# A hybrid decoder trunk with expert retrieval on one core: gate tiles laid out in token pairs, the two routing blocks interleaved, gate steps spread, GpSimd subtractions moved

## The chip, the core and the metric

The kernel runs on one core of a Trainium2 chip. The metric is the device time of one execution in microseconds (us); a time given for a kernel is the median of its runs. The profile is one execution taken by the hardware profiler. Its engines are PE (TensorE: matmuls; PEld is its weight loads), DVE (VectorE), ACT (ScalarE), POOL (GpSimd) and SP (which issues DMAs). Each engine works through its own queue in the order of the program and waits on semaphores for the others.

## What is computed

The network has two layers over 256 tokens of width 1024. Each layer is a token-mixing sublayer (a recurrent, a state-space and an attention group side by side) and a channel-mixing sublayer, the expert retrieval, each followed by a LayerNorm. The change touches the retrieval alone:

```python
def chunk(xc):                                   # 128 tokens
    q = (xc @ wq).reshape(c, PEER_HEADS, 2, half)
    sc = jnp.einsum('thid,ikd->thik', q, keys)   # 8 heads, 2 halves, 128 keys each
    top_s, top_i = lax.top_k(sc, 16)
    cand_s = top_s[:, :, 0, :, None] + top_s[:, :, 1, None, :]
    cand_i = top_i[:, :, 0, :, None] * 128 + top_i[:, :, 1, None, :]
    best_s, best_pos = lax.top_k(cand_s.reshape(c, 8, -1), 16)
    idx = jnp.take_along_axis(cand_i.reshape(c, 8, -1), best_pos, axis=-1)
    gate = jax.nn.softmax(best_s, axis=-1)
    act = gelu(jnp.einsum('td,thkd->thk', xc, u[idx]))
    return jnp.einsum('thk,thkd->td', gate * act, v[idx])
```

So every token picks 8 x 16 of 16,384 experts; the result is the sum over the chosen experts of gate x gelu(x . u) x v.

## The kernel before, in words

The kernel does not gather experts. It computes x . u for all 16,384 of them (the **u stretch**: 128 weight pieces of 128 experts), multiplies by a gate array that is zero where an expert was not chosen, and multiplies by all of v (the **v stretch**: 128 pieces). The array `act` holds [128 first keys, 128 second keys, 256 tokens].

**Weight pieces.** Each piece is 128 x 1024 float32. `pump_split` splits it into a high part `hi` (ACT, L117) and a low part `lo = raw - hi` (L118), up to two pieces ahead (`LOOK`), in three buffers each. L118 stands on DVE, or on POOL for the pieces in the set `on_pool` (L92). A piece of the u stretch is 24 matmuls (`proj_T`, recorded at L193), eight times hi x hTh, hi x hTl and lo x hTh, into one half of a PSUM bank; after two pieces `uevac` applies the GELU on ACT (L977, L980) and, for tokens whose gates are already in place, the product on DVE (L978).

**Background work.** After each u piece the loop takes one or two steps of generators, in this order: routing of token block 0, routing of token block 1, `wgen`.

- `routing(tb)` finds the top 16 of 128 scores for 8 heads x 2 halves (16 searches, L846 to L850), builds 112 candidates per head (L876 to L880), searches them (8 searches), and then makes the choice: exponentials and small index arithmetic (L887 to L903), two one-hot products of 128 x 2048 bf16 (L907 on ACT, L909 and L913 on DVE), 16 small matmuls each, and the transposed key numbers `ijT` and gates `gT`. These are 40 steps.
- `wgen` builds the gate array four tokens at a time (64 groups). `gates` compares key numbers with an iota (L937), multiplies by the gate (L940), and scales a copy (L942), all in half floats on DVE. `wmm` then takes, for each of the four tokens, two 128 x 128 x 128 matmuls (8 in a group), and `apply` puts the result into `act` (DVE L956 for pieces already computed, ACT L958 for the others). A group's gates, matmuls and application stand in three steps that follow each other.

In `eq` and `ga` the four tokens of a group lie next to each other, so the 128 keys that one matmul reads are 4 half floats (8 bytes) apart: `eq[:, 1, :, i]` of a tile [128, 2, 128, 4].

**Order.** The code order is the priority; the framework places each instruction in its engine's queue by that and by its data, so DVE's routing work stands further ahead than the loop's steps say. PE's queue keeps the order of the code. The v stretch begins with `gsplit` of the first four pieces of `act` (ACT L1011, DVE L1012), which write into the buffers of `eq` and `ga`.

Of the kernel before, what the change touches and what calls it, by code (L numbers as in the profile page):

```python
# [16 lines left out]
D = 1024  # L17
# [29 lines left out]
def trunk(ctx, tc, x, wst, ut, vr, pp_d, rb_d, lnrow, bd_d, keys_d, out):  # L47
# [42 lines left out]
    for l in range(DEPTH):  # L90
        on_pool.update(index["w", l, i] for i in (0, 1, 14, 16, 18, N_IN + N_OUT, N_IN + N_OUT + 1))
        on_pool.update(index["u", l, j] for j in range(4, 110, 3))  # L92
# [57 lines left out]
    iota4 = const.tile([128, 128, 4], F16, name="iota4")  # L150
# [19 lines left out]
    def make_consts():  # L170
        POOL.iota(iota4, pattern=[[1, 128], [0, 4]], base=0, channel_multiplier=0, allow_small_or_imprecise_dtypes=True)
# [135 lines left out]
    # (step, token block, part): r residual and sums, m mean and squares, v variance, n reciprocal root, s centre and  # L307
    # gain, o scale and bias with the transposes, l low halves, p the next weight pieces
# [50 lines left out]
    def log1p_exp_neg_abs(pool, o, xin, n, tag):  # L359
        """o = max(x, 0) + log1p(exp(-|x|)) on [128, n]"""  # L360
        a = pool.tile([128, n], F32, name=tag + "_a")
        e = pool.tile([128, n], F32, name=tag + "_e")
        q = pool.tile([128, n], F32, name=tag + "_q")
        ACT.activation(a, xin, AF.Abs)
        ACT.activation(e, a, AF.Exp, scale=-1.0)
        DVE.tensor_scalar(a, e, 2.0, None, op0=OP.add)
        DVE.reciprocal(a, a)
        DVE.tensor_tensor(e, e, a, op=OP.mult)
        DVE.tensor_tensor(a, e, e, op=OP.mult)
        DVE.tensor_scalar(q, a, 1.0 / 17.0, None, op0=OP.mult)  # L370
# [22 lines left out]
    def mixer(l, mix, h, hT, pre):  # L393
# [6 lines left out]
        # small per-layer values  # L400
# [31 lines left out]
        # causal depthwise convolution  # L432
# [293 lines left out]
        # projection schedule  # L726
# [60 lines left out]
        # output projection  # L787
# [33 lines left out]
    def peer(l, pool, hT):  # L821
        hTh, hTl = hT
        act = pool.tile([128, 128, SEQ], F32, name="act")
        ijT = pool.tile([128, 2, SEQ], F16, name="ijT")
        gT = pool.tile([128, 2, SEQ], F16, name="gT")
# [26 lines left out]
        def routing(tb):  # L852
# [19 lines left out]
            for hh in range(8):  # L872
                for i in range(2):
                    top16(tv[:, hh, i, :], ti[:, hh, i, :], sc[:, hh, i, :])
                    yield
# [8 lines left out]
            for hh in range(8):  # L884
                top16(bs[:, hh, :], bp[:, hh * 16:hh * 16 + 16], cand[:, hh, :])
                yield
            DVE.tensor_tensor(ex, bs, bs[:, :, 0:1].to_broadcast([128, 8, 16]), op=OP.subtract)  # L887
# [17 lines left out]
            ts = slice(tb * 128, (tb + 1) * 128)  # L905
            for i in range(2):
# [12 lines left out]
                ACT.activation(ijT[:, i, ts], ps, AF.Copy)  # L919
# [4 lines left out]
            ACT.activation(gT[:, 0, ts], ps, AF.Copy, scale=GS)  # L924
            DVE.scalar_tensor_tensor(gr, ps, GS, gT[:, 0, ts], op0=OP.mult, op1=OP.subtract)
            ACT.activation(gT[:, 1, ts], gr, AF.Copy, scale=LS)
            yield

        state = dict(c=0, t=0)
        TG = 4  # L930
        GS, LS = float(2 ** 15), float(2 ** 11)
# [29 lines left out]
        def wgen():  # L961
            prev = {}
            ng = SEQ // TG
            for i in range(ng + 2):
# [4 lines left out]
                if i >= 2:  # L969
                    apply((i - 2) * TG, prev.pop(i - 2))  # L970
                yield
# [10 lines left out]

        bg = Background()
        bg.add(routing(0))
        bg.add(routing(1))
        bg.add(wgen())
        for jp_ in range(64):
# [7 lines left out]
        # second product  # L995
        po = [[acc_bank() for _ in range(2)] for _ in range(2)]
        early = [[pool.tile([128, w], F32R, name=nm, bufs=2)[:, 0:2 * SEQ] for _ in range(2)]
                 for nm, w in (("eq", 512), ("ga", 768))]
# [151 lines left out]
```

## Time and profile before

| what | value |
|---|---|
| median of 3 runs | 2103.95 us (2101.63 to 2104.25) |
| span of the profiled execution | 2106.6 us |
| PE, PEld busy | 96 %, 87 % |
| DVE, ACT, POOL busy | 73 %, 50 %, 11 % |
| u stretch of layer 0 | 254.46 to 706.42 us |
| u stretch of layer 1 | 1297.10 to 1748.89 us |

Busy shares are means over the whole span; stretches differ. The u stretch has three parts: the routing part (pieces 0 to 53), the gate part (pieces 54 to 117, one group of gates with each piece) and ten pieces without background work. A matmul's record lasts longer than its place in the stream, since matmuls are pipelined: the distance from one start to the next is what a matmul costs.

### The profile page before, as it was taken

How to read it: one execution, taken by the hardware profiler on the slowest of the kernel's cores; microseconds unless marked ns; L12 is line 12 of the kernel's file. 1: busy time of each engine (PE TensorE's matmuls, PEld its weight loads, DVE VectorE, ACT ScalarE, POOL GpSimd, SP SyncE). 2: the span in 40 equal slices, each digit the busy share in tenths (PEclk: the TensorE clock that was granted, in tenths of full speed). 3: DMA queues.
4: the chain of work that ended last, by engine and by line, in shares of the span. 5: the costliest groups of instructions: out<-in, count | busy, mean ns of one | idle time of the engine just before them, and what ended most of it. 6: DMA issues, size and time to landing. Idle time of an engine off the chain costs nothing. (4 is left out here: it accounts for less than half of the span.)

```text
span 2106.6 us, 33808 instructions
## 1 busy us (share of the span) xinstructions
PE 2030.2 (96%) x13212; PEld 1835.5 (87%) x13212; DVE 1548.2 (73%) x2713; ACT 1062.8 (50%) x1523; POOL 238.3 (11%) x120
## 2 busy tenths in 40 slices
PE   7999889999999999999989999899999999999998
PEld 6887889999999888888888769899999998888886
DVE  8786697379999655555687867963999995555555
ACT  5576455454443544444566755554444344444444
POOL 3100122222220000000010001222222200000000
PEclk9999999999999999999999999999999999999999
DMA  6434445544434666666654335455444446666665
GB/s 206 136 110 150 152 152 168 180 141 140 132 130 135 195 194 194 192 194 195 197 180 139 108 133 170 155 173 174 140 132 134 136 151 190 193 196 192 195 195 170
DMA packets 95919, 344.84 MB, mean 164 GB/s; under 512 B 11680, under 2 KB 11952, under 8 KB 95760
## 3 DMA queue, kind: packets, MB, share of 16 engines
q1 hardware_dynamic: 95552, 342.27, 50.3%
q8 instruction: 103, 1.69, 0.3%
q0 software_dynamic: 208, 0.42, 0.1%
q14 instruction: 56, 0.46, 0.1%
HBM read 339.51 MB, written 3.15 MB: 163 GB/s over the span
## 5 line engine op out<-in xcount | busy, mean ns | idle before, releaser
L118 DVE TENSOR_TENSOR lo<-raw,hi 128x1024 fp32r<-128x1024 f32 x544 | 677.5, 1246 | 383.9 <-ACT hi L117 383.5
L117 ACT ACTIVATE hi<-raw 128x1024 fp32r<-128x1024 f32 x630 | 663.8, 1056 | 452.2 <-PE acc L193 342.5
L193 PE MATMUL acc<-hTh,lo 128*128 128x256 f32 x2048 | 581.8, 284 | 20.1 <-DVE lo L118 18.8
L193 PE MATMUL acc<-hTh,hi 128*128 128x256 f32 x2048 | 592.0, 289 | 0.2 <-ACT hi L117 0.2
L193 PE MATMUL acc<-hTl,hi 128*128 128x256 f32 x2048 | 580.1, 283 | 0.0
L193 PEld LDWEIGHTS acc<-hTh,lo 128*128 128x128 f32 x2048 | 392.1, 191 | 24.3 <-DVE lo L118 22.4
L193 PE MATMUL acc<-hi,hTl 128*128 128x512 f32 x1056 | 411.4, 390 | 0.0
L193 PE MATMUL acc<-hi,hTh 128*128 128x512 f32 x1056 | 411.2, 390 | 0.0
L193 PE MATMUL acc<-lo,hTh 128*128 128x512 f32 x1056 | 411.1, 389 | 0.0
L193 PEld LDWEIGHTS acc<-hTh,hi 128*128 128x128 f32 x2048 | 394.3, 193 | 0.7 <-ACT hi L117 0.4
L193 PEld LDWEIGHTS acc<-hTl,hi 128*128 128x128 f32 x2048 | 392.8, 192 | 0.1
L118 POOL TENSOR_TENSOR lo<-raw,hi 128x1024 fp32r<-128x1024 f32 x86 | 223.6, 2602 | 1046.7 <-ACT hi L117 1015.7
L193 PEld LDWEIGHTS acc<-hi,hTh 128*128 128x128 f32 x1056 | 198.3, 188 | 41.6 <-issue 0.7
L193 PEld LDWEIGHTS acc<-hi,hTl 128*128 128x128 f32 x1056 | 198.2, 188 | 41.1
L193 PEld LDWEIGHTS acc<-lo,hTh 128*128 128x128 f32 x1056 | 198.3, 188 | 41.1
L193 PE MATMUL w<-hTh,hi 128*128 128x256 f32 x560 | 161.4, 299 | 7.5 <-DVE y L495 5.7
L1011 ACT ACTIVATE hTh<-act 128x512 fp32r<-128x512 f32 x124 | 77.7, 631 | 166.2 <-PE acc L193 166.2
L1012 DVE TENSOR_TENSOR hTl<-act,hTh 128x512 fp32r<-128x512 f32 x124 | 85.4, 693 | 97.4 <-ACT hTh L1011 97.4
L193 PE MATMUL w<-hTh,lo 128*128 128x256 f32 x560 | 156.9, 289 | 0.0
L193 PE MATMUL w<-hTl,hi 128*128 128x256 f32 x560 | 155.4, 287 | 0.0
L958 ACT ACTIVATE act<-w 128x272 f32<-128x272 f32 (+32 forms) x128 | 61.1, 478 | 146.5 <-DVE act L956 145.8
L193 PE MATMUL w<-eq,ga 128*128 128x128 f16 x512 | 128.0, 294 | 6.9 <-DVE ga L940 6.9
(268 smaller groups left out, 2323.5 us busy)
## 6 DMA issues: line engine op xcount, KB each, us to landing
raw<-in_ut SPq DMA_DIRECT2D x256, 512.0 KB, 3.5
raw<-in_vr SPq DMA_DIRECT2D x256, 512.0 KB, 3.5
raw<-in_wst SPq DMA_DIRECT2D x118, 512.0 KB, 3.5
raw<-in_lnrow SPq DMA_DIRECT2D x8, 512.0 KB, 3.6
hd<-h SPq DMA_DIRECT2D x4, 512.0 KB, 3.9
raw<-hd SPq DMA_DIRECT2D x4, 512.0 KB, 3.5
h<-in_x SPq DMA_DIRECT2D x2, 512.0 KB, 5.7
y<-in_lnrow SPq DMA_DIRECT2D x2, 512.0 KB, 7.0
```

The source lines that it names most:

```text
L117: ACT.activation(hi, raw, AF.Copy)
L118: (POOL if n in on_pool else DVE).tensor_tensor(lo, raw, hi.bitcast(F32), op=OP.subtract)
L193: PE.matmul(ps, lhsT, rhs, start=start, stop=stop)
L958: ACT.activation(v[:, :, c:128], ps[:, :, c:128], AF.Copy, scale=1.0 / GS)
L1011: ACT.activation(gh, src, AF.Copy)
L1012: DVE.tensor_tensor(gl, src, gh.bitcast(F32), op=OP.subtract)
```

## The change

1. `eq` and `ga` become [128, 2, 2, 128, 2]: the tokens of a group lie in two pairs, so the keys that one matmul reads are 2 half floats (4 bytes) apart. The iota, `ijT` and `gT` follow. The scaled copy (L942) goes; the second matmul of a token reads `eq` itself.
2. `routing` is cut into stages. The first block runs search, candidates and their search; then each of the 16 searches of the second block brings one step of the first block's choice with it; the second block's rest follows. That makes 65 steps instead of 80, at 1.5 to a piece as before.
3. After the routing, gate steps are taken at a rate that spreads what is left over all pieces left, instead of one with each piece. Gate matmuls stand with pieces 45 to 124 now (54 to 117 before), with about four pieces in five.
4. `on_pool` holds two of every three pieces from 2 to 50 in the u stretch (33, before: one of three from 4 to 109, 36). From piece 51 on, all low parts are on DVE.

```diff
-        on_pool.update(index["u", l, j] for j in range(4, 110, 3))
+        on_pool.update(index["u", l, j] for j in range(2, 52) if j % 3)
...
         def gates(t0):
-            eq = pool.tile([128, 2, 128, TG], F16, name="eq", bufs=2)
-            A = pool.tile([128, 3, 128, TG], F16, name="ga", bufs=2)
-            sh = [128, 2, 128, TG]
-            DVE.tensor_tensor(eq, iota4[:, None, :, :].to_broadcast(sh),
-                              ijT[:, :, None, t0:t0 + TG].to_broadcast(sh), op=OP.is_equal)
-            DVE.tensor_tensor(A[:, 0:2], eq[:, 0:1].to_broadcast(sh), gT[:, :, None, t0:t0 + TG].to_broadcast(sh),
-                              op=OP.mult)
-            DVE.tensor_scalar(A[:, 2], eq[:, 1], 1.0 / LS, None, op0=OP.mult)
+            g = t0 // TG
+            eq = pool.tile([128, 2, TG // 2, 128, 2], F16, name="eq", bufs=2)
+            A = pool.tile([128, 2, TG // 2, 128, 2], F16, name="ga", bufs=2)
+            sh = [128, TG, 128, 2]
+            def pairs(ap):
+                return ap.rearrange("p c (a e) -> p (c a) e", e=2)[:, :, None, :].to_broadcast(sh)
+            DVE.tensor_tensor(eq.rearrange("p c a k e -> p (c a) k e"), iota2[:, None, :, :].to_broadcast(sh),
+                              pairs(ijT[:, g]), op=OP.is_equal)
+            DVE.tensor_tensor(A.rearrange("p c a k e -> p c (a k) e"),
+                              eq[:, 0].rearrange("p a k e -> p (a k) e")[:, None].to_broadcast([128, 2, TG * 64, 2]),
+                              pairs(gT[:, g]), op=OP.mult)
             return A, eq
...
             for i in range(TG):
-                mm(ps[:, i, :], A[:, 0, :, i], eq[:, 1, :, i], True, False)
-                mm(ps[:, i, :], A[:, 1, :, i], A[:, 2, :, i], False, True)
+                for c in range(2):
+                    mm(ps[:, i, :], A[:, c, i // 2, :, i % 2], eq[:, 1, i // 2, :, i % 2], c == 0, c == 1)
...
+        def route():
+            for stage in range(2):
+                yield from routing(0, stage)
+            choice = routing(0, 2)
+            for _ in routing(1, 0):
+                next(choice, None)
+                yield
+            yield from choice
+            for stage in (1, 2):
+                yield from routing(1, stage)
...
         for jp_ in range(64):
             ps = psum.tile([128, 2, SEQ], F32, name="acc", bufs=4)
             for i in range(2):
-                proj_T(weights(("u", l, jp_ * 2 + i)), hT, ps[:, i, :])
-                bg.step(1 + i if any(g.__name__ == "routing" for g in bg.q) else 1)
+                j = jp_ * 2 + i
+                proj_T(weights(("u", l, j)), hT, ps[:, i, :])
+                if any(g.__name__ == "route" for g in bg.q):
+                    credit += 1.5
+                else:
+                    credit += min(1.0, (SEQ // TG + 3 - state["n"]) / (128 - j))
+                while credit >= 1:
+                    bg.step(1)
+                    credit -= 1
             uevac(jp_, ps)
```

Three places of the queues show the move. The first is DVE's queue in the routing part of layer 0, around the first block's choice. Before, from the low part of piece 9 on, the last candidate search ends and the choice's small operations stand together:

```order
L118 TENSOR_TENSOR lo<-raw,hi 128x1024
L849 MAX act<-act 128x8 x2
L850 MAX_INDEX act<-act 128x8 x2
L846 MAX act<-act 128x8 x2
L847 MAX_INDEX act<-act 128x8 x2
L848 MATCH_REPLACE act<-act 128x112 x2
...
L887 TENSOR_TENSOR act<-act 128x128
L890 TENSOR_SCALAR act<-act 128x128
L891 TENSOR_SCALAR act<-act 128x128
L892 CAST act<-act 128x128
```

After the change, also from the low part of piece 9 on (its line numbers are 2 to 10 higher; the searches are L848 to L852):

```order
L118 TENSOR_TENSOR lo<-raw,hi 128x1024
L849 MAX_INDEX act<-act 128x8
L896 TENSOR_TENSOR act<-act 128x128
L850 MATCH_REPLACE act<-act 128x128
L848 MAX act<-act 128x8
L851 MAX act<-act 128x8
L849 MAX_INDEX act<-act 128x8
L852 MAX_INDEX act<-act 128x8
L850 MATCH_REPLACE act<-act 128x128
L899 TENSOR_SCALAR act<-act 128x128
L851 MAX act<-act 128x8
L900 TENSOR_SCALAR act<-act 128x128
```

The choice's operations now alternate with the second block's searches. All 14 of them and both one-hot operations of the first key (L919, L923) stand between the low parts of pieces 9 and 12. All searches of both blocks stand ahead of the low part of piece 21 now, with 7 low parts between the first search and that one included; before, the same work reached to piece 24, with 15 low parts.

The second place is DVE's queue in the gate part. Before, around the low part of piece 95 of layer 0:

```order
L937 TENSOR_TENSOR eq<-iota_78,ijT 128x1024
L956 SCALAR_TENSOR_TENSOR act<-w,act 128x4x92
L118 TENSOR_TENSOR lo<-raw,hi 128x1024
L940 TENSOR_TENSOR ga<-eq,gT 128x1024
L942 TENSOR_SCALAR ga<-eq 128x512
```

After, at the end of the gate part, with the low parts of pieces 125, 126, 127 and of v pieces 0 to 2 (L952, L954, L970, L993, L1046 are the earlier L937, L940, L956, L978, L1012):

```order
L954 TENSOR_TENSOR ga<-eq,gT 128x1024
L970 SCALAR_TENSOR_TENSOR act<-w,act 128x4x122
L118 TENSOR_TENSOR lo<-raw,hi 128x1024
L993 TENSOR_TENSOR act<-act,acc 128x2x248
L970 SCALAR_TENSOR_TENSOR act<-w,act 128x4x124
L118 TENSOR_TENSOR lo<-raw,hi 128x1024 x2
L993 TENSOR_TENSOR act<-act,acc 128x2x252
L118 TENSOR_TENSOR lo<-raw,hi 128x1024
L970 SCALAR_TENSOR_TENSOR act<-w,act 128x4x126
L118 TENSOR_TENSOR lo<-raw,hi 128x1024
L993 TENSOR_TENSOR act<-act,acc 128x512
L1046 TENSOR_TENSOR eq<-act,eq 128x512
```

The scaled copy is gone, and the last application of gates stands behind the low part of v piece 1.

The third place is ACT's queue at the same end of the u stretch. Before, from the high part of u piece 121 on:

```order
L958 ACTIVATE act<-w 128x4x10
L1011 ACTIVATE eq<-act 128x512
L1011 ACTIVATE ga<-act 128x512
L117 ACTIVATE hi<-raw 128x1024
L977 ACTIVATE acc<-acc 128x512
```

After, from the high part of v piece 2 on (L972, L992, L1045 are the earlier L958, L977, L1011):

```order
L117 ACTIVATE hi<-raw 128x1024
L972 ACTIVATE act<-w 128x4x2
L992 ACTIVATE acc<-acc 128x512
L1045 ACTIVATE eq<-act 128x512
L1045 ACTIVATE ga<-act 128x512
```

The first splits of `act` for the v stretch stood four pairs of pieces ahead of the end; now they stand behind the last GELU and behind v piece 2's high part.

## Rows read from the trace of the kernel before

**Rows 1.** The page, part 1: busy time, share of the span, instructions.

```profile
PE 2030.2 (96%) x13212; PEld 1835.5 (87%) x13212; DVE 1548.2 (73%) x2713; ACT 1062.8 (50%) x1523; POOL 238.3 (11%) x120
```

**Rows 2.** Busy time by window: length, PE, PEld, DVE, ACT, POOL, clock, DMA, GB/s.

```profile
254.46:427.53 173.07, 163.58 (x1365) 161.49 (x1364) 120.87 (x440) 84.74 (x100) 44.59 (x18) 0.99 0.50 159
427.53:677.54 250.01, 246.27 (x2051) 241.27 (x2049) 236.58 (x324) 110.24 (x188) 49.19 (x19) 1.00 0.42 135
1297.10:1470.84 173.74, 162.87 (x1365) 160.19 (x1363) 122.09 (x440) 84.50 (x100) 43.76 (x18) 1.00 0.48 158
1470.84:1720.01 249.17, 246.03 (x2050) 241.24 (x2049) 235.69 (x324) 110.20 (x188) 50.04 (x19) 1.00 0.41 135
362.17:405.37 43.20, 43.20 (x362) 43.20 (x361) 12.25 (x10) 19.76 (x23) 11.96 (x5) 1.00 0.61 187
457.90:519.10 61.20, 61.20 (x515) 60.33 (x514) 56.31 (x81) 30.12 (x50) 15.78 (x6) 1.00 0.42 137
```

**Rows 3.** Waits of PE in layer 0's two parts: us, times, longest.

```profile
PE acc L193 <- DVE lo L118: 8.8, 8, 2.1
...
PE w L193 <- DVE ga L940: 3.7, 6, 0.9
```

**Rows 4.** Timeline of PE, one group's gate matmuls: start, length, instruction.

```profile
461.03 0.29 PE L193 MATMUL w<-eq,ga 128*128 128x128 f16 x1
...
461.85 0.29 PE L193 MATMUL w<-ga 128*128 128x128 f16 x1
461.89 0.37 PE L193 MATMUL acc<-hTh,hi 128*128 128x256 f32 x1
```

**Rows 5.** Timeline of PE, the 16 matmuls of a one-hot product.

```profile
411.13 1.07 PE L193 MATMUL w<-identb,act 128*128 128x128 bf16 x16
412.01 0.36 PE L193 MATMUL acc<-hTh,hi 128*128 128x256 f32 x1
```

**Rows 6.** Groups by form, weight loads: busy us, mean ns, idle before.

```profile
L193 PEld LDWEIGHTS <-ga 128*128 128x128 f16 x1024 | 104.1, 118 | 16.4 <-DVE ga L940 9.5
...
L193 PEld LDWEIGHTS <-act 128*128 128x128 bf16 x128 | 7.2, 98 | 0.3
```

**Rows 7.** By line, gate part of layer 0: shortest, median, longest ns.

```profile
L937 DVE TENSOR_TENSOR eq<-iota,ijT x62: 671/686/2850, 431.4 to 673.5; 128x1024 f16<-128x1024 f16 x62
...
L940 DVE TENSOR_TENSOR ga<-eq,gT x62: 672/684/2883, 433.2 to 675.8; 128x1024 f16<-128x1024 f16 x62
...
L942 DVE TENSOR_SCALAR ga<-eq x62: 273/282/325, 433.8 to 676.4; 128x512 f16<-128x512 f16 x62
...
L118 DVE TENSOR_TENSOR lo<-raw,hi x45: 1204/1224/1258, 428.7 to 674.1; 128x1024 fp32r<-128x1024 f32 x45
L118 POOL TENSOR_TENSOR lo<-raw,hi x19: 2390/2650/3483, 425.8 to 637.6; 128x1024 fp32r<-128x1024 f32 x19
```

**Rows 8.** Timeline of DVE, routing part: first two pairs of searches, piece 24's low part.

```profile
250.04 0.48 DVE L846 MAX8 act<-act 128x8 f32<-128x128 f32 x2
...
252.39 0.47 DVE L846 MAX8 act<-act 128x8 f32<-128x128 f32 x2
...
335.51 1.21 DVE L118 TENSOR_TENSOR lo<-raw,hi 128x1024 fp32r<-128x1024 f32 x1
```

**Rows 9.** Timeline of POOL and DVE, low parts of pieces 7 and 6.

```profile
270.29 2.39 POOL L118 TENSOR_TENSOR lo<-raw,hi 128x1024 fp32r<-128x1024 f32 x1 [5.99 <-ACT hi L117]
270.51 3.26 DVE L118 TENSOR_TENSOR lo<-raw,hi 128x1024 fp32r<-128x1024 f32 x1
```

**Rows 10.** Timeline of PE and ACT where u goes over into v, layer 0.

```profile
706.42 0.40 PE L193 MATMUL acc<-hi,eq 128*128 128x512 f32 x1
706.50 1.06 ACT L117 ACTIVATE hi<-raw 128x1024 fp32r<-128x1024 f32 x1 [1.82 <-PE acc L193]
...
707.47 0.58 ACT L977 ACTIVATE acc<-acc 128x512 f32<-128x512 f32 x1
707.98 2.17 ACT L1011 ACTIVATE hTh<-act 128x512 fp32r<-128x512 f32 x4
```

More of the change, by code (lines that the diff above doesn't have):

```diff
@@ L149, in trunk @@
     POOL.tensor_scalar(ident, jp, 0.0, None, op0=OP.is_equal)
-    iota4 = const.tile([128, 128, 4], F16, name="iota4")
+    iota2 = const.tile([128, 128, 2], F16, name="iota2")
     iota16 = const.tile([128, 16, 16], BF16, name="iota16")
@@ L170, in make_consts @@
     def make_consts():
-        POOL.iota(iota4, pattern=[[1, 128], [0, 4]], base=0, channel_multiplier=0, allow_small_or_imprecise_dtypes=True)
+        POOL.iota(iota2, pattern=[[1, 128], [0, 2]], base=0, channel_multiplier=0, allow_small_or_imprecise_dtypes=True)
         POOL.iota(iota16, pattern=[[1, 16], [0, 16]], base=0, channel_multiplier=0, allow_small_or_imprecise_dtypes=True)
@@ L823, in peer @@
         act = pool.tile([128, 128, SEQ], F32, name="act")
-        ijT = pool.tile([128, 2, SEQ], F16, name="ijT")
-        gT = pool.tile([128, 2, SEQ], F16, name="gT")
+        TG = 4
+        ijT = pool.tile([128, SEQ // TG, 2, TG], F16, name="ijT")
+        gT = pool.tile([128, SEQ // TG, 2, TG], F16, name="gT")
         def view(slot, n):
@@ L850, in top16, with routing @@
             DVE.max_index(idx[:, 8:16], vals[:, 8:16], src)
-        def routing(tb):
+        def routing(tb, stage):
             base = 92
@@ L871, in routing @@
             sc = scs[tb]
[L872 to L875, printed above, removed]
+            if stage == 0:
+                for hh in range(8):
+                    for i in range(2):
+                        top16(tv[:, hh, i, :], ti[:, hh, i, :], sc[:, hh, i, :])
+                        yield
+                return
+            if stage == 2:
+                yield from select(tb, tf, pab, bs, bp, px, py, fx, fy, fp, sm, ex, gr, oh, tx)
+                return
             DVE.tensor_copy(tf, ti)
@@ L886, in routing, with select @@
                 yield
+        def select(tb, tf, pab, bs, bp, px, py, fx, fy, fp, sm, ex, gr, oh, tx):
             DVE.tensor_tensor(ex, bs, bs[:, :, 0:1].to_broadcast([128, 8, 16]), op=OP.subtract)
@@ L904, in routing @@
             yield
-            ts = slice(tb * 128, (tb + 1) * 128)
+            gs = slice(tb * 128 // TG, (tb + 1) * 128 // TG)
+            grp = lambda ap: ap.rearrange("p (g t) -> p g t", t=TG)
             for i in range(2):
@@ L918, in routing @@
                     mm(ps, oh[:, a, :], identb, a == 0, a == 15)
-                ACT.activation(ijT[:, i, ts], ps, AF.Copy)
+                ACT.activation(ijT[:, gs, i, :], grp(ps), AF.Copy)
                 yield
@@ L923, in routing @@
             yield
-            ACT.activation(gT[:, 0, ts], ps, AF.Copy, scale=GS)
-            DVE.scalar_tensor_tensor(gr, ps, GS, gT[:, 0, ts], op0=OP.mult, op1=OP.subtract)
-            ACT.activation(gT[:, 1, ts], gr, AF.Copy, scale=LS)
+            ACT.activation(gT[:, gs, 0, :], grp(ps), AF.Copy, scale=GS)
+            DVE.scalar_tensor_tensor(grp(gr), grp(ps), GS, gT[:, gs, 0, :], op0=OP.mult, op1=OP.subtract)
+            ACT.activation(gT[:, gs, 1, :], grp(gr), AF.Copy)
             yield
-        state = dict(c=0, t=0)
-        TG = 4
-        GS, LS = float(2 ** 15), float(2 ** 11)
+        state = dict(c=0, t=0, n=0)
+        GS = float(2 ** 15)
         def gates(t0):
-            eq = pool.tile([128, 2, 128, TG], F16, name="eq", bufs=2)
-            A = pool.tile([128, 3, 128, TG], F16, name="ga", bufs=2)
-            sh = [128, 2, 128, TG]
-            DVE.tensor_tensor(eq, iota4[:, None, :, :].to_broadcast(sh),
-                              ijT[:, :, None, t0:t0 + TG].to_broadcast(sh), op=OP.is_equal)
-            DVE.tensor_tensor(A[:, 0:2], eq[:, 0:1].to_broadcast(sh), gT[:, :, None, t0:t0 + TG].to_broadcast(sh),
-                              op=OP.mult)
-            DVE.tensor_scalar(A[:, 2], eq[:, 1], 1.0 / LS, None, op0=OP.mult)
+            g = t0 // TG
[9 more added lines that the diff above has]
+                              pairs(gT[:, g]), op=OP.mult)
             return A, eq
@@ L970, in wgen @@
                     apply((i - 2) * TG, prev.pop(i - 2))
+                state["n"] = i + 1
                 yield
@@ L981, in uevac @@
             state["c"] = j + 2
+        def route():
[4 more added lines that the diff above has]
+                next(choice, None)
+                yield
+            yield from choice
+            for stage in (1, 2):
+                yield from routing(1, stage)
         bg = Background()
-        bg.add(routing(0))
-        bg.add(routing(1))
+        bg.add(route())
         bg.add(wgen())
+        credit = 0.0
         for jp_ in range(64):
@@ L996, in peer @@
         po = [[acc_bank() for _ in range(2)] for _ in range(2)]
-        early = [[pool.tile([128, w], F32R, name=nm, bufs=2)[:, 0:2 * SEQ] for _ in range(2)]
-                 for nm, w in (("eq", 512), ("ga", 768))]
+        early = [[pool.tile([128, w], F32R, name=nm, bufs=2) for _ in range(2)]
+                 for nm, w in (("eq", 512), ("ga", 512))]
         ring = []
```

## The prediction

> **What bounds the kernel now.** I read the page first, for the bound: PE is busy in 96% of the span, DVE in 73% [rows 1]. So only two things can shorten the span, matmuls that cost less and time in which PE stands still. I then cut both u stretches into their parts with the busy times by window [rows 2] and asked what a part would take if PE never waited.
>
> Between 362.17 and 405.37 us fifteen pieces pass without any background matmul in 43.20 us [rows 2]: 2.88 us a piece, 0.120 us for each of its 24 matmuls of 256 columns. Between 457.90 and 519.10 us sixteen pieces, each with a group of gates, take 61.20 us: 3.825 us a piece, PE busy throughout. So the 8 gate matmuls cost 3.825 - 2.88 = 0.945 us, 0.118 us each. The timeline agrees: from the first to the eighth start 0.82 us pass, 0.117 each [rows 4].
>
> The 16 small matmuls of the one-hot product are the comparison. They too have 128 columns and 128 x 128 weights of two bytes, but lie without gaps, and take from 411.13 to 412.01 us [rows 5]: 0.88 us, 0.055 us each. A gate matmul costs twice as much for the same arithmetic.
>
> Now the standstill. Routing part, layer 0: 54 pieces x 2.88 = 155.5 us, plus four one-hot products at 0.88 and two transposes, 3.7 us, make 159.2; it takes 173.07 [rows 2], so 13.9 us are lost (layer 1: 14.5). Gate part: 64 x 3.825 = 244.8 against 250.01, 5.2 us lost (layer 1: 4.4). The waits name who is late: DVE's low parts in the first part, DVE's gate product in the second [rows 3].
>
> **The change, part by part, for one layer.**
>
> *Gate matmuls in pairs.* 512 matmuls stay; only the spacing of the half floats they read changes, from 8 bytes to 4. No row has a half-float operand 4 bytes apart, so I bound it. Above: 0.118 us, nothing gained. Below: 0.055 us, as without gaps. The row it is nearest to is the ordinary piece: its float32 operand is read in steps of 4 bytes, and its 256 columns cost 0.120 us, 0.47 ns a column, against 0.92 ns for the gate matmul and 0.43 ns for the one-hot product. Four bytes apart is therefore a spacing at which PE is seen at full speed. The weight load is not what holds the gate matmul: 118 ns against 98 ns for the bf16 tile [rows 6]. I take 0.057 us. Saved: 512 x 0.061 = **31.2 us**.
>
> A page speaks against this term. The Trainium skill (SBUF — State Buffer, section "Specifications (TRN2)") says that SBUF lines are 16 bytes and that two hits on a line are enough for full bandwidth. A spacing of 8 bytes gives two hits, so by that rule the old layout already ran at full speed and the sum would lose this term. The two spacings just read, 0.117 and 0.055 us [rows 4, 5], don't fit it: two hits a line go along with half the speed here, and the measurement decides.
>
> *The scaled copy goes.* 64 x 0.28 us of DVE [rows 7], hidden behind matmuls except in the 5.2 us of waits; it has no price of its own.
>
> *GpSimd out of the gate part.* When POOL holds a subtraction, DVE's operation on SBUF tensors stands until it is over: the low part of piece 6 starts 0.22 us after POOL's and takes 3.26 us instead of 1.2 [rows 9]. The gate operations show it at large: median 686 and 684 ns, longest 2850 and 2883 [rows 7]. POOL spent 49.19 us there on 19 low parts [rows 2, 7]; DVE will spend 19 x 1.22 = 23 us on them and not be held. DVE's load per piece, with the steps spread, is then: low part 1.14 (its place in the stream), four gate groups in five pieces x (0.60 + 0.60 + 0.5 to 1.2 for the application), and 0.1 to 0.3 for the product: 2.6 rising to 3.4 us. PE needs 2.88 + 0.8 x 8 x 0.057 = 3.24. So DVE is above PE only over the last dozen pieces, by 0.1 to 0.2 us each, some 2 us in all, and low parts two pieces ahead cover that. I count **-4.8 us** (the mean of 5.2 and 4.4) for the waits removed and **+1.0** for what DVE's narrow margin costs; were the cover gone it would be 2 to 5.
>
> *The routing part.* Searches are untouched: a pair takes 252.39 - 250.04 = 2.35 us [rows 8]. In layer 0 DVE works without a break from 250.04 to the end of piece 24's low part, 336.72 us, and PE wanted that one at 254.46 + 24 x 2.88 + 0.88 + 0.24 = 324.7: 12.0 us late. Of these 86.7 us, 15 low parts are 17.1, the 48 searches 56, blocking behind POOL about 4.8 (2.0 for piece 6 alone), the rest 8.8. After the change all that, and one us more of the second choice, stands ahead of piece 21, with 7 low parts: 56 + 9.6 + 8.0 = 73.6 us from 249.8, that is 323.4. PE wants it at 254.46 + 21 x 2.88 + 0.24 = 315.2. That is 8.2 us late before any blocking. Blocking grows: 14 POOL subtractions instead of 7 in that stretch, and the small operations of the choice, which read and write SBUF as the low part does, now alternate with searches, so each POOL subtraction that meets them costs DVE some 2 us. Four such meetings are 8 us. If none met, the route would lose 8 (6 us gained against 13.9); if nearly all did, 22. I take 16: **+2.0 us**.
>
> *Gate steps spread to the end.* Before, PE goes from u to v without a pause [rows 10], since the first splits of `act` were done. Now the last application and the last GELU come first. In ACT's queue stand, from PE's last u matmul on: v piece 2's high part (starts 0.08 us after it, 1.06 long), a small copy 0.2, the GELU 0.58, the split 0.61 (the three durations: [rows 10]). The first v matmul waits for all of them: **+2.6 us** (1 to 4). DVE's half of the split is due 1.6 us later, seven matmuls on, and should make it.
>
> **Sum.** -31.2 - 4.8 + 1.0 + 2.0 + 2.6 = -30.4 us a layer, -61 for both. The profiled execution's span is 2106.6 us, 2.65 above the median of the runs; against the median, 2103.95 - 61 = **2043 us**.
>
> **The rivals.**
>
> *A, no faster matmul.* The gate matmul stays at 0.118 us: whatever slows it is not the spacing, or 4 bytes are as bad as 8. For it: no row shows a strided half-float operand at full speed. Against: the float32 rows. Then the rest remains, -4.8 + 2.0 + 2.6 = -0.2 us a layer (the margin costs nothing, PE needing 3.6 us a piece): about 2103 us, 2090 to 2116 with the bounds of the routing part. The rule of the Trainium skill (SBUF — State Buffer) weighed above leads here.
>
> *B, half of it.* The weight load or the moving operand alone gains: 0.08 to 0.10 us, 10 to 20 us a layer saved instead of 31, 2065 to 2087 us.
>
> *C, slower: DVE loses its fast rate on pairs.* The gate operations take 1024 half floats in 0.68 us, the low part 1024 float32 in 1.22 [rows 7]. The inner run falls from four half floats to two; if that costs the fast rate, an operation takes 1.2 us and DVE becomes the bound of the gate part. Its load there is 236 us from piece 43 on (85 low parts x 1.14, 64 applications, the products, 128 gate operations x 0.60) and PE's 274. At 1.22 us a gate operation it is 315, 41 above PE: -30.4 + 41 = +10.6 us a layer, 2125 us. It decides from 1.13 us on, where the 30.4 us are used up. Against it: the one-hot operations of the routing and the present gates keep the rate with broadcast operands, and a run of two half floats is still a whole 4 bytes.
>
> *D, routing much worse.* If every choice operation meets POOL (22 us lost, the upper end above), a layer loses 8 us more than now instead of 2: 2055 us with the faster matmul. It changes the size, not the sign, and lies in the forecast's own range.
>
> **Chances.** The forecast 0.78, and with all bounds taken to one side (routing -6 to +8, margin 0 to 5, tail 1 to 4) its own range is 2022 to 2066; A 0.10; B 0.06; C 0.06. A difference within 0.2% (4 us) can't be told from no change. Faster: 0.78 + 0.06, 0.04 of A and 0.01 of C, 0.89. Same: 0.03 of A and 0.01 of C, 0.04. Slower: 0.03 of A and 0.04 of C, 0.07. The range 2022 to 2087 takes in the forecast and B and leaves out A, C and a tail: just under two in ten.
>
> **What the profile after would show.** Gate matmuls 0.055 to 0.060 us apart, pieces with gates 3.34 us (right); 0.11 or more (A). Gate operations with a longest value near the median from piece 51 on, and a median of 0.68 (right) or above 1.1 us (C). First low part that PE waits for at pieces 6 to 9, the last at 21, some 16 us lost by piece 24. A pause of 2 to 3 us before the first v matmul. The prediction is wrong above all if the matmul spacing does not move.

## The result, and the profile after

The changed kernel takes 2051.03 us (median of four runs, 2049.66 to 2058.22) against 2104.10 us before on the same chip: a ratio of 0.9753, 95% interval 0.9733 to 0.9773. That is 53 us less where 61 were forecast. The span of the profiled execution is 2047.9 us. The page's first part, then five windows (both u stretches in two parts, and the pause at the end of layer 0's), answer to [rows 1, 2]:

```profile
PE 1974.3 (96%) x13212; PEld 1785.6 (87%) x13212; DVE 1482.5 (72%) x2599; ACT 1072.0 (52%) x1539; POOL 216.8 (11%) x114
```

```profile
250.32:401.76 151.44, 139.91 (x1148) 138.22 (x1147) 103.26 (x415) 73.15 (x87) 72.02 (x29) 0.95 0.47 150
401.76:674.08 272.32, 272.32 (x2506) 269.52 (x2504) 240.68 (x308) 139.47 (x227) 8.76 (x4) 1.00 0.50 161
674.08:676.42 2.34, 0.16 (x2) 0.00 (x0) 1.90 (x2) 2.21 (x5) 0.00 (x0) 1.00 0.62 201
1264.34:1415.66 151.32, 138.60 (x1148) 136.99 (x1147) 103.35 (x415) 73.26 (x87) 71.89 (x29) 0.97 0.46 150
1415.66:1687.98 272.32, 272.32 (x2506) 269.52 (x2504) 240.76 (x308) 139.59 (x227) 8.75 (x4) 1.00 0.50 161
```

The routing part has 45 pieces now, the rest 83, with all 64 groups of gates. In the rest PE is busy for all of 272.32 us in both layers. In the routing part it stands for 151.44 - 139.91 = 11.5 us. From the first u to the first v matmul layer 0 takes 426.10 us (451.96 before) and layer 1 425.98 (451.79): 25.9 and 25.8 us less, 51.7 together. This distance, **u to v** below, repeats from layer to layer to within about 1 us; the stretches around it vary between executions (with the same code ahead of it, the first u matmul of layer 0 stood at 249.6 to 256.7 us), so single runs are compared by it.

The gate matmuls of two groups, on PE's timeline, answer to [rows 4]:

```profile
500.12 0.64 PE L193 MATMUL w<-eq,ga 128*128 128x128 f16 x8
500.56 0.36 PE L193 MATMUL acc<-hTh,hi 128*128 128x256 f32 x1
500.76 0.28 PE L193 MATMUL acc<-hTl,hi 128*128 128x256 f32 x1
...
503.52 0.64 PE L193 MATMUL w<-eq,ga 128*128 128x128 f16 x8
```

Eight gate matmuls take 0.44 us up to the next ordinary one (0.86 before), 0.055 each, and a piece with gates 3.40 us (3.825 before). The first ordinary matmul behind a group takes 0.20 us up to the next one instead of 0.12 (0.21 before).

PE's waits in layer 0's routing part (us, times, longest; [rows 3]); from there to the end of the u stretch PE waits for nothing:

```profile
PE acc L193 <- DVE lo L118: 7.1, 3, 5.4
PE acc L193 <- POOL lo L118: 3.6, 3, 1.9
PE acc L193 <- ACT hi L117: 0.8, 1, 0.8
```

The gate operations from 425 us on, where POOL has no low part any more (shortest, median, longest ns; [rows 7]):

```profile
L952 DVE TENSOR_TENSOR eq<-iota,ijT x57: 672/691/726, 425.3 to 660.5; 128x1024 f16<-128x1024 f16 x57
...
L954 DVE TENSOR_TENSOR ga<-eq,gT x57: 672/685/727, 427.2 to 662.3; 128x1024 f16<-128x1024 f16 x57
```

None of them is held now; the longest was 2883 ns before.

ACT and PE where u goes over into v ([rows 10]). The first v matmul comes 2.34 us later than the stream would have it, behind the very four instructions that the prediction lists:

```profile
674.21 1.06 ACT L117 ACTIVATE hi<-raw 128x1024 fp32r<-128x1024 f32 x1 [1.76 <-issue]
675.17 0.17 ACT L972 ACTIVATE act<-w 128x8 f32<-128x8 f32 x1
675.23 0.60 ACT L992 ACTIVATE acc<-acc 128x512 f32<-128x512 f32 x1
675.75 0.62 ACT L1045 ACTIVATE eq<-act 128x512 fp32r<-128x512 f32 x1
...
676.42 0.50 PE L193 MATMUL acc<-hi,eq 128*128 128x512 f32 x1 [2.18 <-ACT eq L1045]
```

### The profile page after: what moved, and what is told of

It reads as the page before. It is cut to its first block, busy times and chain, and to the rows that moved or that the text cites. A ratio compares the mean times of both kernels' runs of the same rounds, so it can differ in the third digit from the quotient of the medians.

```text
span 2047.9 us, 33528 instructions
## 1 busy us (share of the span) xinstructions
PE 1974.3 (96%) x13212; PEld 1785.6 (87%) x13212; DVE 1482.5 (72%) x2599; ACT 1072.0 (52%) x1539; POOL 216.8 (11%) x114
## 3 DMA queue, kind: packets, MB, share of 16 engines
q1 hardware_dynamic: 95552, 342.27, 51.7%
## 5 line engine op out<-in xcount | busy, mean ns | idle before, releaser
L118 POOL TENSOR_TENSOR lo<-raw,hi 128x1024 fp32r<-128x1024 f32 x80 | 201.9, 2531 | 621.0 <-ACT hi L117 591.8
L1045 ACT ACTIVATE hTh<-act 128x512 fp32r<-128x512 f32 x124 | 77.7, 631 | 166.2 <-PE acc L193 166.2
L1046 DVE TENSOR_TENSOR hTl<-act,hTh 128x512 fp32r<-128x512 f32 x124 | 85.4, 693 | 97.3 <-ACT hTh L1045 97.3
L970 DVE SCALAR_TENSOR_TENSOR act<-w,act 128x224 f32<-128x224 f32 (+35 forms) x128 | 122.3, 956 | 8.2 <-ACT act L995 8.1
L193 PEld LDWEIGHTS w<-hTh,hi 128*128 128x128 f32 x560 | 109.0, 200 | 10.1 <-issue 6.1
```

Of the source, the lines that this page charges most:

```text
L118: (POOL if n in on_pool else DVE).tensor_tensor(lo, raw, hi.bitcast(F32), op=OP.subtract)
L193: PE.matmul(ps, lhsT, rhs, start=start, stop=stop)
L970: DVE.scalar_tensor_tensor(v[:, :, 0:c], ps[:, :, 0:c], 1.0 / GS, v[:, :, 0:c], op0=OP.mult, op1=OP.mult)
L1045: ACT.activation(gh, src, AF.Copy)
L1046: DVE.tensor_tensor(gl, src, gh.bitcast(F32), op=OP.subtract)
```

## The experiments

All runs in one table; intervals where a kernel was timed in rounds, one run otherwise. The kernel before took 2103.8 to 2105.7 us beside them.

| kernel | us | ratio to before (95%) | u to v, layers 0 and 1 |
|---|---|---|---|
| before | 2104.10 | 1 | 451.96, 451.79 |
| changed | 2051.03 | 0.9733 to 0.9773 | 426.10, 425.98 |
| x_quads | 2112.23 | 1.0011 to 1.0041 | 453.19, 453.00 |
| x_moving8 | 2112.60 | one run | 453.10, 452.14 |
| x_stationary8 | 2060.98 | one run | 428.59, 427.86 |
| x_unit | 2127.44 | one run | 463.51, 463.55 |
| b_pairs | 2073.11 | 0.9838 to 0.9889 | 434.77, 435.84 |
| x_sequence | 2049.59 | one run | 425.00, 424.96 |
| x_rate1 | 2050.68 | one run | 423.77, 423.64 |
| x_pool_third | 2049.46 | one run | 423.64, 424.20 |
| x_pool_old | 2057.55 | one run | 425.64, 426.29 |
| x_tail | 2052.38 | 0.9736 to 0.9775 | 423.78, 423.63 |
| y_scores | 2037.59 | 0.9656 to 0.9703 | 421.44, 421.56 |
| y_ln | 2039.43 | 0.9663 to 0.9697 | 421.53, 421.10 |

### Is it the spacing, and of which operand?

**x_quads**: the changed kernel with the old layout of eight bytes, still without the scaled copy.

```diff
-            eq = pool.tile([128, 2, TG // 2, 128, 2], F16, name="eq", bufs=2)
+            eq = pool.tile([128, 2, 128, TG], F16, name="eq", bufs=2)
...
-                    mm(ps[:, i, :], A[:, c, i // 2, :, i % 2], eq[:, 1, i // 2, :, i % 2], c == 0, c == 1)
+                    mm(ps[:, i, :], A[:, c, :, i], eq[:, 1, :, i], c == 0, c == 1)
```

> The changed kernel with the old layout of the gate tiles alone (four tokens side by side, keys 8 bytes apart); the scaled copy stays away, order, POOL placement and spreading stay as changed. If the spacing sets the cost of a gate matmul: 0.117 to 0.120 us each again instead of 0.065, 512 x 0.053 = 27 us a layer more, 2051 + 54 = 2105 us. If the gain came from DVE (copy gone, GpSimd out of the gate part, steps spread): the matmuls stay near 0.065 us, or PE's u stretch stays within 5 us, 2045 to 2060 us.

Two groups on its PE timeline:

```profile
505.61 1.11 PE L193 MATMUL w<-eq,ga 128*128 128x128 f16 x8
506.47 0.37 PE L193 MATMUL acc<-hTh,hi 128*128 128x256 f32 x1
...
509.43 1.11 PE L193 MATMUL w<-eq,ga 128*128 128x128 f16 x8
```

0.86 us for eight again, 3.82 us a piece, and the whole gain is gone. Without the layout the rest of the change together gains nothing. (Its ten runs spread from 2103 to 2115 us, and the traced one took 2103.43. Its u to v is 1.2 us longer than before in each layer, which is what the other terms measured below make without the matmuls: -5.2 + 4.2 + 2.3 = +1.3 in layer 0.)

**x_moving8** and **x_stationary8** put only one of the two operands back to eight bytes. Both also split the key comparison on DVE into two operations, one for each layout (0.42 us each).

```diff
...
-                    mm(ps[:, i, :], A[:, c, i // 2, :, i % 2], eq[:, 1, i // 2, :, i % 2], c == 0, c == 1)
+                    mm(ps[:, i, :], A[:, c, i // 2, :, i % 2], eq[:, 1].rearrange("p a k e -> p (a k e)").rearrange("p (k t) -> p k t", t=TG)[:, :, i], c == 0, c == 1)
```

```diff
...
-                    mm(ps[:, i, :], A[:, c, i // 2, :, i % 2], eq[:, 1, i // 2, :, i % 2], c == 0, c == 1)
+                    mm(ps[:, i, :], A[:, c, :, i], eq[:, 1, i // 2, :, i % 2], c == 0, c == 1)
```

> Only the moving operand of the gate matmuls (the second key's one-hot) 8 bytes apart, the stationary one stays at 4. If the moving operand sets the rate: 0.115 to 0.120 us a matmul, u stretch 27 us longer. If the weight load does: 0.065 us as changed. If each costs half: about 0.09 us.

> Only the stationary operand of the gate matmuls (the gates) 8 bytes apart, the moving one stays at 4. If the moving operand sets the rate: 0.065 us or a little more, u stretch as changed. If the weight load does: 0.115 to 0.120 us, u stretch 27 us longer. If each costs half: about 0.09 us.

A group on the PE timeline of x_moving8, then of x_stationary8:

```profile
502.36 1.09 PE L193 MATMUL w<-eq,ga 128*128 128x128 f16 x8
503.20 0.37 PE L193 MATMUL acc<-hTh,hi 128*128 128x256 f32 x1
```

```profile
504.75 0.66 PE L193 MATMUL w<-eq,ga 128*128 128x128 f16 x8
505.21 0.36 PE L193 MATMUL acc<-hTh,hi 128*128 128x256 f32 x1
```

0.84 us with the moving operand eight bytes apart, 0.46 to 0.48 with the stationary one. The moving operand sets the rate; the stationary one costs about 2 us a layer. x_stationary8's single run is 10 us above the changed kernel's median, but its two u-to-v distances are together only 4.4 us longer, and its first u matmul came 3.4 us later, in code that the edit doesn't touch.

**x_unit** lays the keys of a token without gaps, so the two operations that make gates have their token operand broadcast along the innermost dimension.

```diff
-            eq = pool.tile([128, 2, TG // 2, 128, 2], F16, name="eq", bufs=2)
+            eq = pool.tile([128, 2, TG, 128], F16, name="eq", bufs=2)
...
+                              gT[:, g][:, :, :, None].to_broadcast([128, 2, TG, 128]), op=OP.mult)
```

> The changed kernel with each token's keys side by side (2 bytes apart), gate operations with a broadcast innermost dimension. Spacing theory: gate matmuls 0.055 to 0.058 us apart, 4 us a layer less on PE. For DVE two theories: the fast rate needs a run in every operand, then 1.1 to 1.2 us a gate operation instead of 0.68, DVE bounds the gate part and the u stretch grows by 25 to 40 us (2100 to 2130 us); or the rate does not depend on it, then 0.68 us and about 2043 us.

One group on its PE timeline, the gate product in its gate part by line, and that part by window:

```profile
505.13 0.62 PE L193 MATMUL w<-eq,ga 128*128 128x128 f16 x8
505.56 0.36 PE L193 MATMUL acc<-hTh,hi 128*128 128x256 f32 x1
```

```profile
L955 DVE TENSOR_TENSOR ga<-eq,gT x62: 1204/1206/2947, 411.8 to 704.1; 128x1024 f16<-128x1024 f16 x62
```

```profile
406.00:712.65 306.65, 284.48 (x2506) 269.89 (x2504) 303.07 (x308) 138.90 (x229) 9.90 (x4) 1.00 0.43 141
```

Without gaps a group takes 0.43 us, so four bytes apart was already full speed for PE (0.44). But DVE's operations go from 0.684 to 1.206 us, DVE is busy 303.07 of 306.65 us, and u to v becomes 463.5 us. This is what rival C priced, at +10.6 us a layer and 2125 us; here it is +11.6 and 2127.44. That it comes so close is in part luck: of the 41 us that DVE was to add to the gate part 34.3 are there (306.65 against 272.32 us), and the gain they were set against was 25.9 us, not 30.4. The Trainium skill (VectorE: DVE Perf Modes, section "What auto-detection actually checks") says that the two-a-cycle rate wants every tensor to be 16-bit with step 1 or -1. The two durations agree: a run of two keeps step 1, the broadcast along the innermost dimension does not.

### What the other three parts are worth

**b_pairs** is the kernel before with the pair layout and without the scaled copy, nothing else.

> The kernel before with the pair layout alone (and so without the scaled copy); order, one step with each piece and POOL placement as before. If the spacing gives the whole gain: PE needs 27 us a layer less, but DVE with POOL in the gate part stands at 3.6 to 4.0 us a piece against PE's 3.40 and becomes late: 10 to 20 us of it are lost again, about 2065 to 2085 us. If DVE is not in the way: 2104 - 54 = 2050 us. If the spacing gives nothing by itself: 2095 to 2105 us.

Its PE's waits in the gate part of layer 0, and the window from piece 54 to the end of u:

```profile
PE w L193 <- DVE ga L946: 11.2, 17, 1.7
```

```profile
422.90:684.52 261.62, 250.05 (x2290) 243.57 (x2290) 239.41 (x282) 123.57 (x209) 51.07 (x19) 1.00 0.46 150
```

The layout, with the scaled copy gone, gives 31 us of the 53 (the copy gone without the layout is in x_quads, which gains nothing). Once PE is faster, one group with each piece and POOL's low parts between leave DVE behind: PE waits 11.2 us for the gate product, against 3.7 before [rows 3].

**x_sequence** routes the blocks one after the other, **x_rate1** takes one gate step a piece, **x_pool_third** leaves POOL one low part in three up to piece 49, **x_pool_old** one in three from 4 to 109 as before.

```diff
-            for stage in range(2):
-                yield from routing(0, stage)
...
-            yield from choice
-            for stage in (1, 2):
-                yield from routing(1, stage)
+            for tb in range(2):
+                for stage in range(3):
+                    yield from routing(tb, stage)
```

```diff
-                    credit += min(1.0, (SEQ // TG + 3 - state["n"]) / (128 - j))
+                    credit += 1.0
```

```diff
-        on_pool.update(index["u", l, j] for j in range(2, 52) if j % 3)
+        on_pool.update(index["u", l, j] for j in range(4, 52, 3))
```

```diff
-        on_pool.update(index["u", l, j] for j in range(2, 52) if j % 3)
+        on_pool.update(index["u", l, j] for j in range(4, 110, 3))
```

> The changed kernel with the two blocks' routing one after the other again (80 steps), POOL placement as changed. If the choice's small operations between searches meet POOL and that is what made the routing part lose 18 us a layer instead of 14: the loss falls below 14 us. If the loss is DVE's plain backlog of searches ahead of piece 21 or 24: it stays at 14 to 19 us. The gate part starts later (piece 54), so its steps stand closer; the span would be 2045 to 2055 us either way.

> The changed kernel with one gate step after each piece again instead of spreading them to the end. DVE's load per piece is then up to 3.9 us against 3.40 of PE: if spreading is what keeps DVE ahead, the gate part waits 10 to 20 us a layer; the pause of 2.2 us before the first v matmul goes. If the faster gate operations alone suffice: no waits and 2 us a layer less than the changed kernel.

> The changed kernel with POOL taking one low part in three of pieces 4 to 49 (16) instead of two in three (33), none later. DVE gets 17 low parts more, 19 us, in the routing part. If blocking by POOL is what made the routing part worse: loss 14 us or less a layer. If POOL relieves DVE on balance: loss above 18 us, up to 26.

> The changed kernel with the old POOL placement (one in three of pieces 4 to 109). If POOL in the gate part costs PE: gate operations up to 2.8 us again, 20 low parts of DVE less (24 us) against some 30 us of blocking, and with PE at 3.3 us a piece DVE gets late: 5 to 15 us a layer more in the gate part. If it was harmless: the gate part stays without a wait.

Undone one at a time, none of these parts costs anything in u to v: three come out 1.0 to 2.5 us a layer shorter, x_pool_old the same (of its 6.5 us more, 6.2 lie ahead of layer 0's first u matmul, at 256.47 us). Undone all together they cost 9 to 10 us a layer (b_pairs). So they cover for each other. With the steps spread, POOL may stay in the gate part (x_pool_old's PE waits 1.7 us there); with POOL out, the steps need not be spread (x_rate1's waits for nothing). No run undoes two of the three parts, so which two are enough stays open.

Two of these runs also bear on the routing part. x_sequence still loses 18.1 us there, the wait of 5.4 us for piece 21's low part included, and four of its choice operations take 2.4 us each beside a GpSimd subtraction, as many as in the changed kernel. So the order of the blocks is not what makes the routing part worse. PE's waits in x_pool_third's routing part, and that part by window:

```profile
PE acc L193 <- DVE lo L118: 10.8, 10, 2.0
```

```profile
250.35:399.33 148.98, 138.11 (x1148) 135.63 (x1147) 115.03 (x432) 73.11 (x87) 38.12 (x15) 0.99 0.47 153
```

It loses 148.98 - 133.3 = 15.7 us (133.3 us is the work of that part, worked out below), between the two outcomes expected. Its waits add up to nearly as much as the changed kernel's (10.8 us against 11.5), but none is longer than 2.0 us, and the clock was granted at 0.99 instead of 0.95.

### The pause before v, and the routing

**x_tail** ends the gate steps some seven pieces earlier. **y_scores** does that too and issues the second block's score matmuls inside the routing, so that its searches can't stand ahead of early low parts.

```diff
-                    credit += min(1.0, (SEQ // TG + 3 - state["n"]) / (128 - j))
+                    credit += min(1.0, (SEQ // TG + 3 - state["n"]) / max(1, 120 - j))
```

```diff
...
-            for _ in routing(1, 0):
+            scores(1, 0)
+            for n, _ in enumerate(routing(1, 0)):
+                if n % 4 == 1 and n < 12:
+                    scores(1, n // 4 + 1)
                 next(choice, None)
```

> The changed kernel with the gate steps finished some seven pieces earlier. The pause of 2.2 us before the first v matmul goes from both layers: 4 us less than the changed kernel, about 2046 us, if DVE stays ahead at its higher load (3.2 to 3.6 us against 3.40 a piece). If DVE becomes late instead: no gain or up to 5 us more.

> As the run with an early end of the gate steps, and the second block's score matmuls are issued in the routing (from piece 17 on) instead of before it, so that its searches can't stand in DVE's queue ahead of early low parts. If the 18 us lost in the routing part are DVE's searches ahead of the low parts of pieces 3 to 21: the loss falls to 4 to 8 us, about 2020 to 2028 us. If they are POOL's blocking or the choice's chain through ACT and PE: 14 to 18 us stay lost, about 2040 to 2047 us.

In x_tail the pause is gone, 2.3 us a layer, and the median is no better: from the first v matmul of layer 0 to the first u matmul of layer 1 593.39 us pass instead of 587.92 (the same 593.39 in x_rate1, which has no pause either). The time comes back at the LayerNorms. The last pair of DVE operations of the one behind v and POOL's first low parts for layer 1, in the changed kernel and then in x_tail:

```profile
1030.07 1.42 DVE L273 SCALAR_TENSOR_TENSOR h<-sz,ln_nw,raw 128x512 f32<-128x512 f32 x2
...
1030.88 2.83 POOL L118 TENSOR_TENSOR lo<-raw,hi 128x1024 fp32r<-128x1024 f32 x1 [22.42 <-DVE h L273]
```

```profile
1027.73 3.51 DVE L273 SCALAR_TENSOR_TENSOR h<-sz,ln_nw,raw 128x512 f32<-128x512 f32 x2
...
1028.23 5.25 POOL L118 TENSOR_TENSOR lo<-raw,hi 128x1024 fp32r<-128x1024 f32 x2 [21.93 <-ACT hi L117]
```

POOL starts 0.81 us after the pair's start in the one and 0.50 us after it in the other; by those 0.3 us it falls ahead of the pair's second half, which then stands behind it, and the pair takes 2.1 us longer. The LayerNorm ahead of layer 1's u stretch shows the same, 1.41 and 3.51 us. PE's waits for the LayerNorms show how many such pairs a kernel has behind the first LayerNorm: 28.1 to 28.3 us with none (the changed kernel, x_quads, x_sequence), 30.0 to 30.5 with one, 32.4 to 32.7 with two (x_tail). Behind layer 0's v stretch the pair is long in all kernels that go from u to v without a pause (before, b_pairs, x_rate1, x_tail, y_scores; y_ln below moves the subtraction) and in x_unit with 0.3 us of it, and short in six of the seven with a longer one; x_pool_third has the pause of 2.2 us and the long pair all the same. Other LayerNorms have it too, such as the one ahead of layer 0's u stretch (before, x_pool_old, y_scores), where no pause lies ahead. So a pause goes along with the short pair but does not decide it; that is a matter of tenths of a microsecond.

y_scores beats both kernels (its four runs spread from 2034.6 to 2040.5 us, and the traced one took 2040.47). PE's waits in its routing part, and that part by window (with 16 more matmul records, which took 3.4 us ahead of the stretch in the changed kernel):

```profile
PE acc L193 <- POOL lo L118: 6.3, 6, 2.1
PE acc L193 <- DVE lo L118: 1.0, 1, 1.0
PE acc L193 <- ACT hi L117: 0.7, 2, 0.6
```

```profile
250.88:400.00 149.12, 141.09 (x1165) 138.55 (x1163) 102.76 (x438) 75.14 (x91) 74.38 (x30) 0.99 0.48 156
```

The wait for DVE's low parts fell from 7.1 to 1.0 us: the backlog in DVE's queue was the cause of it. POOL's low parts come late in its place, 6.3 us instead of 3.6, which the expectation left out. So 149.12 - 133.3 - 3.4 = 12.4 us are lost there, between the two outcomes expected, and so is the median.

**y_ln** is y_scores with the first two low parts behind each LayerNorm but the first on DVE, in its order behind the LayerNorm's last pair (q0, q1).

```diff
...
+                def low(n=n, lo=lo, raw=raw, hi=hi, eng=POOL if n in on_pool and late is None else DVE):
+                    eng.tensor_tensor(lo, raw, hi.bitcast(F32), op=OP.subtract)
...
-        seq("r00 r01 m0 s00 s01 v0 r10 n00 r11 n01 m1 n02 n03 o00 v1 o01 s10 n10 s11 n11 n12 n13 p1 o10 o11 l00 l01 l10 l11 p2"),
+        seq("r00 r01 m0 s00 s01 v0 r10 n00 r11 n01 m1 n02 n03 o00 v1 o01 s10 n10 s11 n11 n12 n13 p1 o10 o11 q0 l00 l01 l10 l11 q1 p2"),
```

> The kernel of y_scores with the first two low parts behind each LayerNorm (but the first one) taken by DVE, in its own order behind the LayerNorm's last two operations, instead of by GpSimd beside them. Theory (a pause ahead of the v stretch is given back in the LayerNorm: without the pause a GpSimd low part meets the LayerNorm's last pair of DVE operations, which then take 3.51 us instead of 1.42): the pair takes 1.42 us at every place; PE's waits for the LayerNorm's output fall from 32.4 us to 28 or 29, about as in the changed kernel with its pause (28.2); against that PE may wait up to 1 us at each of three places for the two low parts. Net -2 to -5 us: a median of 2033 to 2036 us where y_scores had 2037.6. Rival (the low parts on DVE are as much in the way as on GpSimd, or the LayerNorm's waits differ by chance of the execution): 2037 to 2041 us, with a new wait for these low parts or for the third operand behind them.

The pair takes 1.42 us and PE's waits for the LayerNorms fall from 32.4 to 29.4 us, as the theory says; the median doesn't move, as the rival says (the five runs, 2038.4 to 2040.0 us, lie inside the spread of y_scores), and of the new waits that the rival names PE has 1.4 us for the third operand (`hTl`). Windows of 5 us, 5 to 20 us after the last v matmul of layer 0, in y_scores and then in y_ln:

```profile
1025.55:1030.55 5.00, 2.11 (x9) 1.72 (x10) 4.90 (x7) 2.33 (x3) 4.07 (x2) 0.55 0.45 129
1030.55:1035.55 5.00, 5.00 (x34) 4.87 (x34) 3.00 (x5) 2.37 (x4) 1.19 (x1) 0.76 0.93 309
1035.55:1040.55 5.00, 5.00 (x44) 5.00 (x44) 3.74 (x6) 3.49 (x5) 0.00 (x0) 1.00 0.54 186
```

```profile
1022.80:1027.80 5.00, 3.24 (x14) 2.87 (x15) 4.89 (x10) 3.89 (x5) 0.00 (x0) 0.50 0.70 220
1027.80:1032.80 5.00, 5.00 (x28) 5.00 (x28) 2.93 (x4) 0.78 (x2) 0.00 (x0) 0.57 0.69 236
1032.80:1037.80 5.00, 5.00 (x44) 5.00 (x43) 4.27 (x8) 3.26 (x5) 0.00 (x0) 1.00 0.51 173
```

PE begins earlier in y_ln (14 matmuls against 9 in the first window), but at half clock for longer: 28 against 34 in the second. After three windows it has begun 86 against 87. Behind this LayerNorm the granted clock took back what the shorter pair gave.

## Why the prediction was right, and what was mis-sized

The forecast's mechanism held, and none of the rivals came. Per layer, layer 0 first:

- **Gate matmuls in pairs**, forecast -31.2 us, measured -27.2 (64 x (3.825 - 3.40)). The spacing was forecast at 0.057 us and is 0.055. What was mis-sized is the price of the old ones: "3.825 - 2.88 = 0.945 us, 0.118 us each" charged the eight matmuls with the 0.08 us that the first ordinary matmul behind a group loses. It loses them after the change too. The row was there: from the first gate matmul to the next ordinary one 0.86 us pass [rows 4], 0.108 each. This makes the sum 4 us a layer too large, 8 of the 9 us between the forecast 61 and the 51.7 of u to v. The rule of the Trainium skill (SBUF — State Buffer, section "Specifications (TRN2)"), by which two hits on a line of 16 bytes are enough, does not hold for the moving operand here: 0.84 us a group at eight bytes, 0.44 at four.
- **Waits of the gate part**, forecast -4.8 and +1.0 for DVE's margin; measured -5.2 and -4.4, and 0. PE is busy throughout, so the cover held to the last dozen pieces. The prediction gave these waits to POOL leaving and the copy going; x_pool_old, where POOL stays, has only 1.7 us of them, so most of them go without POOL leaving.
- **Routing part**, forecast +2.0 (16 us lost instead of 14); measured 18.1 lost instead of 13.9, and 18.0 instead of 14.5: +4.2 and +3.5. DVE's lateness came as forecast. Four of the choice's operations stand beside a GpSimd subtraction for 2.0 to 2.4 us instead of 0.2 to 0.3 (the first two below), and when the low part of piece 21 comes, 327.19 - 250.32 - 21 x 2.88 - 0.24 = 16.1 us are lost:

```profile
281.87 2.25 DVE L907 SCALAR_TENSOR_TENSOR act<-act 128x128 f32<-128x128 f32 x1
...
284.24 2.20 DVE L908 CAST act<-act 128x128 bf16<-128x128 f32 x1
```

```profile
327.19 0.58 PE L193 MATMUL acc<-hTh,lo 128*128 128x256 f32 x1 [5.38 <-DVE lo L118]
```

  What was mis-sized is what the 16 was set against. It is the lateness at one low part, and for the kernel before the prediction has that as 12.0 us; it took the 13.9 of the whole part. Like for like the term is +4. And the split of the waits was not foreseen: all of PE's waits grew by 2.0 us in layer 0 (11.5 against 173.07 - 163.58 = 9.5 [rows 2]) and by 1.8 in layer 1 (12.7 against 10.9), but those for DVE's low parts fell (8.8 to 7.1, and 10.0 to 9.4), while those for POOL's own rose from 0.7 to 3.6 and 2.6. The rest is PE's busy time, 139.91 us for work of 45 x 2.88 + 3.7 = 133.3, so 6.6 too much against 4.4 before (5.3 against 3.7). The granted clock was 0.95 and 0.97 there, 0.99 and 1.00 before.
- **Pause before v**, forecast +2.6, measured +2.34, in the order foretold. That the kernels without it (x_tail, x_rate1) are no faster in the end, since their LayerNorms cost as much more, was not foreseen.

Sum: -27.2 - 5.2 + 4.2 + 2.3 = -25.9 in layer 0, -25.8 in layer 1, 51.7 for both. That the matmuls alone make nearly the whole miss is luck: the routing part, forecast 1.9 us a layer too low, is offset for the most part by DVE's margin and the pause, 1.3 too high. The medians differ by 53.1, and the stretches outside u to v differ between executions by more than the rest. The marks foretold for the profile: gate operations at 0.685 and 0.691 us with none held (right); the last low part that PE waits for at piece 21 (the wait of 5.4 us, right); the first at pieces 6 to 9 (piece 7, right, but it is POOL's); pieces with gates 3.34 us (3.40: the 0.08 just named). By the prediction's own terms rival A's range begins at 2088 us, not 2090.

The clock in layer 0's routing part shows in windows of three pieces' time, 26 to 43 and 69 to 86 us after its start, with an undisturbed one between:

```profile
276.24:284.88 8.64, 5.72 (x41) 5.11 (x40) 8.64 (x36) 5.51 (x7) 3.27 (x2) 0.90 0.23 83
284.88:293.52 8.64, 8.64 (x54) 8.57 (x54) 8.64 (x29) 2.17 (x2) 1.47 (x1) 0.70 0.39 126
...
302.16:310.80 8.64, 8.64 (x74) 8.64 (x74) 8.57 (x50) 3.66 (x4) 5.18 (x3) 1.00 0.59 182
...
319.44:328.08 8.64, 3.26 (x24) 3.05 (x23) 7.43 (x14) 1.81 (x3) 4.73 (x2) 0.77 0.00 1
328.08:336.72 8.64, 8.64 (x71) 8.60 (x71) 3.79 (x4) 2.90 (x5) 0.05 (x1) 0.83 0.68 240
```

Each time PE first stands (5.72 and 3.26 us busy of 8.64), and the clock falls from 2.4 to 1.2 GHz for a part of that window or the next; where PE is busy again throughout, at 0.70, 54 matmuls pass instead of 74. x_pool_third, whose waits are as much in sum but shorter, agrees: 0.99, and 138.11 us busy for the same work.

## What to carry to other kernels

Price an operation by the change in the length of a whole period, but split off what the switch to and from it costs, since that stays when the operation gets faster. Lay half floats that a matmul streams at most four bytes apart, and keep an inner run of two for the engine that writes them, so that both keep their rate. Where several edits guard against one shortage, undo them singly and together: alone, each looks worthless.

## What was not expected of the hardware

- A wait of PE costs more than its length: after the stops in the routing part the clock was granted at 0.70 to 0.90 of full speed in stretches of 8.64 us, and PE's busy time exceeds its work by 2 us a layer more than before. Behind the LayerNorm of layer 0 an earlier start of PE (y_ln) was used up by a clock that stayed low longer.
- The operand that streams and the operand that is loaded differ: eight bytes apart costs a group 0.84 us in the one and 0.46 in the other, against 0.44.
- Whether a GpSimd subtraction falls into the LayerNorm's last pair (3.51 or 1.42 us) turned on 0.3 us between the changed kernel and x_tail. Why the clock came back at 10 us behind the last v matmul in the changed kernel and at 15 in x_tail stays open; no run changed that alone.
